# An encoder layer on one core: low parts of attention's weights on either engine, gates and fillers re-spread, the last two heads kept on chip, and the last projection's products in another order

## The chip, the cores and the metric
One Trainium2 chip, one of its cores. The metric is the device time of one execution in microseconds; the kernel's times are medians of several runs on the same chip.

## The reference
One layer of a streaming encoder, for 1024 prompt tokens and 32 new tokens that continue a cache of 512 (together T = 1056 token columns), model width 1024, 8 + 8 heads of 64, feed-forward width 4096, all in float32.

```python
h = rmsnorm(x)
z = h @ w_in                       # q,k,v of mixer A; indexer q,k,w; q,k,v of mixer B; gate_a, gate_b
# mixer A, per head: softmax(q k^T / 8) v over the top 256 keys that the indexer picks (a mask)
# mixer B, per head: a = exp(log_sigmoid(s) - sum of softplus(s) of the later keys); a v, causal
m = sigmoid(gate_a) * (o_a @ w_branch_a) + sigmoid(gate_b) * (o_b @ w_branch_b)
y = x + m @ w_out                  # then, with u = relu(rmsnorm(y) @ w_up) ** 2:
out = y + u @ w_down
```

## The kernel before
Every float32 product is made of three products of float32r parts: each operand x is split into a high part xh (a ScalarE cast) and a low part xl = x - xh (a subtraction), and `three` adds wh xh + wh xl + wl xh in one PSUM bank. A piece of weights is 128x512: `unit` loads it into `wst`, `split` makes `wh` on ScalarE and `wl` on the engine that `self.low` names. That is GpSimd from the start, and "either" from the feed-forward on.

The kernel doesn't issue instructions in the order of its code. `Plan` records each one with a rank (FAST, PREP, MAIN, FILL, SLOW) and then issues by its own estimated clock: on each engine the ready instruction of the lowest rank goes first. For an instruction of "either" it compares when VectorE and when GpSimd would be done with it (VectorE gets it if it would be done over 500 ns sooner: `dve + LEAN < pool`). What it decides is fixed in the program, so each engine runs its list in order and waits where the estimate was too early.

The stages, in the order of time, with the microsecond of the profile at which each begins: projections, indexer and top-k (0), mixer B's attention (465), mixer A's (685), merge with the gates (912), w_out (936), w_up (1029), w_down (1359).

Attention goes head by head (`attend`): two queries' blocks of scores (`s` banks), weights from them on ScalarE, VectorE and GpSimd, transposes (`t` banks), and products with v (`o` banks). `halves` adds the two halves of an `o` bank on ScalarE and VectorE into a tile `o`, which a DMA stores to `do` in HBM. Mixer A goes through its eight heads twice: pass 0 for the first 512 queries, pass 1 for the rest. A head's k, v and q come from HBM into rings of 3, 3 and 2 tiles. The few queries of the new tokens go with heads 2 and 5 (`attend_new`).

Between heads TensorE is given fillers (rank FILL, bank `pj`): gates (`gate`, 72 matmuls each, two pieces of `w_g`), and the branch products of finished heads, `branch_b0`, `branch_b1` and `branch_a0` (12, 24 and 12 matmuls). Four tables say how many are recorded where: `GATES_FIRST` ahead of mixer B's first head, `GATES_BESIDE[h]` behind B's head h, `FILL_AHEAD` ahead of mixer A, and `FILL_BESIDE` behind each head of A, pass 0 first. Fillers of A are held until the head before them is done (`behind`). The first `branch_b0` comes with `load_o`, which reads B's outputs from `do`. The last `load_o` brings A's outputs of the second half into `xl` for the merge.

The last projection (`down`) makes seven products per quarter of the output, by a scheme that saves one of eight. The inner dimension has 16 pieces of u. A stage goes over four quarters q; in its first quarter it loads the forms of u that it needs (`load`: a DMA, a cast on ScalarE, a subtraction on either engine, 128x528 each) into a ring of 24 slots, and keeps them for the other three. The stages are, in order: B11 (16 forms), the trio T2, T3, B22 over the first 8 pieces (24 forms) and over the other 8 (24 forms), B21 (16 forms), and the pair T1, T4 over 8 and 8 pieces (16 forms each). One unit is 24 matmuls: 4 pieces by two column blocks of 256 and 272 by 3 products. The trio's weights are sums and differences that VectorE makes (`us<-us`). `finish` multiplies a ready block, adds the residual from `dh` (ring `self.hs`) and stores it.

Of the kernel before, what the change touches and what calls it, by code (L numbers as in the profile page):

```python
# [10 lines left out]
F32 = mybir.dt.float32  # L11
# [12 lines left out]
SEQ = 1024  # L24
DEC = 32
PAST = 512
T = SEQ + DEC
# [19 lines left out]
GATES_BEFORE, GATES_FIRST = 4, 4  # L47
GATES_BESIDE = (1,1,1,1,1,1,0,0)
FILL_BESIDE = (0,1,1,1,2,2,2,2,2,2,2,2,2,2,2,1)
# [58 lines left out]
class Plan:  # L108
# [3 lines left out]
    def __init__(self, nc, tc):  # L112
        self.nc, self.tc = nc, tc
        self.tensor, self.vector = Issuer(self, PE, nc.tensor), Issuer(self, DVE, nc.vector)
        self.scalar, self.gpsimd = Issuer(self, ACT, nc.scalar), Issuer(self, POOL, nc.gpsimd)
        self.sync = Issuer(self, SP, nc.sync)
        self.either = Issuer(self, EITHER, nc)
        self.nodes, self.mem, self.rings = [], {}, {}
        self.members, self.banks, self.onchip = {}, set(), set()
# [31 lines left out]
    def open(self, name, side="left", space=None):  # L151
# [6 lines left out]
        self.members[name] = []  # L158
        return p
# [9 lines left out]
    def tile(self, pool, shape, dtype, name, tag=None, bufs=1, fine=False):  # L169
# [8 lines left out]
        if kw:  # L178
# [3 lines left out]
            m = Mem(1 if psum else 4, 1 if psum else words, old, self.floors[pool[2]])  # L182
# [277 lines left out]
class Layer:  # L460
# [103 lines left out]
    def run(self):  # L564
# [98 lines left out]

        self.att = self.pr = nc.open("att", "right")
# [542 lines left out]
    def attend(self, h, is_a, passes=(0, 1)):  # L1207

        nc, at = self.nc, self.att
        g = h if is_a else H + h  # L1210
        kk = nc.tile(at, [128, SEQ], F32R, "k", bufs=3)
# [27 lines left out]
        for i in passes:  # L1239
            o = nc.tile(at, [64, 512], F32, "o", bufs=2)  # L1240
            for t0 in (4 * i + 2, 4 * i):
# [22 lines left out]
                self.halves(po, o[:, c:c + 256])  # L1264
            with nc.rank(FAST):
                nc.sync.dma_start(self.do[g, :, 512 * i:512 * i + 512], o)
# [82 lines left out]
    def load_o(self, o, g, groups):  # L1349

        nc = self.nc
        for e in range(4):
            for i in groups:
                lo, hi = ((0, W1), (W1, T))[i]
                h, l = o[i][:, e], o[i][:, 4 + e]
                with nc.rank(PREP):
                    nc.sync.dma_start(
                        l.bitcast(F32), self.do[2 * g + 2 * e:2 * g + 2 * e + 2, :, lo:hi].rearrange("g e t -> (g e) t"))
                    nc.scalar.copy(h, l.bitcast(F32))
                    nc.gpsimd.tensor_sub(l, l.bitcast(F32), h.bitcast(F32))  # L1360
# [275 lines left out]
    def down(self, late, form):  # L1636
# [7 lines left out]
        self.hs = self.ring(self.temps(self.ft, 4, 0, 512))  # L1644
# [61 lines left out]
        for fs, weights, blocks, after in (  # L1706
                ((B11,), one(0, 0), (range(16),), after1),
                ((T2, T3, B22), weights6, (range(8), range(8, 16)), after6),
                ((B21,), one(0, 1), (range(16),), after2),
                ((T1, T4), weights5, (range(8), range(8, 16)), after5)):  # L1710
            for b, block in enumerate(blocks):
                u = {}
                for q in range(4):
                    tags = [next(self.turn) for _ in fs]
                    ps = [[self.bank(t)[:, :n] for n, _ in QUADS] for t in tags]
                    for p0, ws in [(p0, weights(q, p0 // 4)) for p0 in range(block[0], block[-1], 4)]:
                        for f, w, bank in zip(fs, ws, ps):
                            wh, wl = w()
                            if q == 0:
                                u.update({(f, p): load(f, p) for p in range(p0, p0 + 4)})  # L1720
                            for i, (n, lo) in enumerate(QUADS):
                                cs = slice(i * 256, i * 256 + n)
                                with nc.rank(FILL):
                                    for s in range(4):
                                        ks = slice(s * 128, s * 128 + 128)
                                        uh, ul = (z[:, cs] for z in u[f, p0 + s])
                                        self.three(bank[i], wh[:, ks], wl[:, ks], uh, ul,
                                                   p0 + s == block[0], p0 + s == block[-1])
                    for i, (n, lo) in enumerate(QUADS):

                        def d(r, c, done=False, q=q, n=n, lo=lo):
                            cs = slice(lo + c * n, lo + c * n + n)
                            if done:
                                return self.finish(2 * q + r, cs)
                            return self.pick(self.yy, 2 * q + r, cs)

                        with nc.rank(FAST):
                            after(b, d, *(z[i] for z in ps))
# [96 lines left out]
```

## Time and profile before

| | us |
|---|---|
| median of 3 runs (1704.97 to 1709.24) | 1705.32 |
| the profiled execution | 1703.88 |
| its span, first to last instruction | 1702.1 |
| TensorE busy with matmuls in the span | 1671.8 (98%) |
| VectorE, ScalarE, GpSimd busy | 1349.7, 942.4, 847.7 |

A matmul's busy time runs from its start to a modelled end and is longer than the time until the next may start, so a busy share near 100% doesn't say that TensorE issues at its pace. The share of its weight loads (PEld) falls with every wait, and so does the number of matmuls in a window of fixed length. L440 is the one line in which `Plan` issues everything, so instructions are told apart by their tiles: out<-in.

### The profile page before, as it was taken

The page shows a single profiled execution, that of the slowest core. Times are in us where ns is not written, and L with a number is a line of the kernel's source. Part 1 is how long each engine was busy: PE and PEld are TensorE (multiplying, and loading weights), DVE is VectorE, ACT ScalarE, POOL GpSimd, SP SyncE. Part 2 cuts the span into 40 slices and gives each one's busy share as a digit, 9 for nine tenths or more (in the row PEclk, how much of TensorE's full clock was granted, in tenths as well). Part 3 has the DMA queues.
Part 4 walks back from the last instruction along what each step waited for, and adds up shares of the span by engine and source line. Part 5 has one row for each costly group of instructions (what it writes and reads, how often), then busy time and mean ns, then how long its engine had stood idle before and what let it go on. Part 6 is the DMA issues. An engine that isn't in the chain of part 4 may idle for free.

```text
span 1702.1 us, 34820 instructions
## 1 busy us (share of the span) xinstructions
PE 1671.8 (98%) x12242; PEld 1591.3 (93%) x12242; DVE 1349.7 (79%) x2846; ACT 942.4 (55%) x2019; POOL 847.7 (50%) x699
## 2 busy tenths in 40 slices
PE   8999999999999999899999999999999999999998
PEld 7998999999999998798999999999999999989998
DVE  8777899987477888876666549999988879888756
ACT  7556888764376776877754555333333544425431
POOL 5432332343386676456668648433333556656420
PEclk9999999999999999999999999999999999999999
DMA  7234453355573636778855644444443687756744
GB/s 257 83 104 125 140 154 121 103 157 149 156 213 94 188 97 166 197 237 241 241 178 160 182 122 134 156 140 140 140 150 130 225 274 237 271 161 235 252 131 149
DMA packets 182575, 289.00 MB, mean 170 GB/s; under 512 B 30976, under 2 KB 62176, under 8 KB 182400
## 3 DMA queue, kind: packets, MB, share of 16 engines
q1 hardware_dynamic: 182112, 286.43, 54.4%
q8 instruction: 97, 1.59, 0.4%
q14 instruction: 78, 0.64, 0.1%
q10 hardware_dynamic: 288, 0.34, 0.1%
HBM read 193.52 MB, written 93.07 MB: 168 GB/s over the span
## 4 chain that ended last, share of the span: by engine, by line
PE 85%; DVE 8%; issue 2%; DMA 2%; ACT 1%; POOL 1%; SPq 0%; DVEq 0%; ACTq 0%; POOLq 0%
PE pj L440 35%; PE c L440 11%; PE b L440 10%; PE a L440 10%; PE s L440 10%; PE o L440 5%; PE t L440 5%; DVE junk L440 2%; DVE y L440 1%; DVE mh L440 1%; DVE us L440 1%; POOL wl L440 0%; SPq L440 0%; DVE wl L440 0%; DVE small L440 0%
## 5 line engine op out<-in xcount | busy, mean ns | idle before, releaser
L440 PE MATMUL pj<-xl,wh 128*128 128x272 f32 (+2 forms) x1200 | 335.5, 312 | 0.0
L440 POOL TENSOR_TENSOR wl<-wst,wh 128x512 fp32r<-128x512 f32 x160 | 231.5, 1455 | 200.8 <-ACT wh L440 195.1
L440 PE MATMUL pj<-xh,wh 128*128 128x272 f32 (+1 forms) x768 | 251.6, 328 | 0.0
L440 PE MATMUL pj<-xh,wl 128*128 128x272 f32 (+1 forms) x768 | 250.8, 327 | 0.2 <-POOL wl L440 0.2
L440 PEld LDWEIGHTS pj<-xl,wh 128*128 128x128 f32 x1200 | 212.9, 188 | 10.5
L440 ACT CAST wh<-wst 128x512 fp32r<-128x512 f32 x213 | 130.4, 620 | 132.0 <-PE a L440 21.9
L440 PEld LDWEIGHTS pj<-xh,wl 128*128 128x128 f32 x768 | 144.5, 188 | 11.1 <-POOL wl L440 0.5
L440 PEld LDWEIGHTS pj<-xh,wh 128*128 128x128 f32 x768 | 144.6, 188 | 10.2 <-DVE gz L440 0.3
L440 POOL TENSOR_TENSOR p<-p,rem 128x383 f32<-128x383 f32 (+8 forms) x66 | 101.8, 1562 | 45.3 <-DVE rem L440 34.3
L440 DVE TENSOR_TENSOR tt<-t,tt 128x512 fp32r<-128x512 f32 (+2 forms) x168 | 101.4, 621 | 26.4 <-ACT tt L440 25.5
L440 POOL TENSOR_TENSOR wl<-y,wh 128x512 fp32r<-128x512 f32 x49 | 73.2, 1496 | 95.9 <-ACT wh L440 92.8
L440 DVE TENSOR_TENSOR_SCAN rem<-rem,first 128x384 f32<-128x384 f32 (+8 forms) x66 | 113.9, 1748 | 7.5 <-ACT rem L440 6.3
L440 ACT CAST tt<-t 128x512 fp32r<-128x512 f32 (+2 forms) x168 | 86.9, 539 | 42.0 <-PE t L440 34.6
L440 ACT CAST wh<-y 128x512 fp32r<-128x512 f32 x79 | 49.1, 622 | 105.9 <-issue 23.0
L440 ACT ACTIVATE junk<-score,cand 128x1024 bf16<-128x1024 f32 (+2 forms) x93 | 97.0, 1043 | 12.3 <-DVE cand L440 10.7
L440 PE MATMUL s<-k,q 128*128 128x512 f32 (+4 forms) x384 | 97.9, 353 | 5.6 <-DVE nb L440 3.0
L440 ACT CAST wh<-us 128x512 fp32r<-128x512 f32 x64 | 39.6, 622 | 114.1 <-PE pj L440 27.6
L440 PE MATMUL o<-tt,v 128*128 128x256 f32 (+1 forms) x640 | 98.4, 279 | 0.8 <-DVE o L440 0.4
L440 PEld LDWEIGHTS o<-tt,v 128*128 128x128 f32 x640 | 89.9, 189 | 6.3 <-DVE o L440 0.7
L440 DVE TENSOR_SCALAR_CACHE_REDUCE junk<-score,cand 128x384 bf16<-128x384 f32 (+1 forms) x124 | 92.9, 749 | 3.1
L440 PE MATMUL t<-ident,p 128*128 128x128 f32 (+1 forms) x596 | 90.9, 275 | 0.2 <-DVE tt L440 0.2
L440 POOL TENSOR_TENSOR wl<-us,wh 128x512 fp32r<-128x512 f32 x33 | 49.7, 1515 | 72.6 <-ACT wh L440 72.6
(359 smaller groups left out, 5610.3 us busy)
## 6 DMA issues: line engine op xcount, KB each, us to landing
us<-w_down SPq DMA_DIRECT2D x80, 256.0 KB, 3.0
q<-dq SPq DMA_DIRECT2D x64, 256.0 KB, 4.5
du<-y SPq DMA_DIRECT2D x56, 264.0 KB, 2.5
du<-us SPq DMA_DIRECT2D x56, 264.0 KB, 2.5
y<-w_up SPq DMA_DIRECT2D x44, 256.0 KB, 2.7
k<-dk SPq DMA_DIRECT2D x40, 256.0 KB, 5.0
v<-dv SPq DMA_DIRECT2D x40, 256.0 KB, 4.3
xl<-du SPq DMA_DIRECT2D x35, 264.0 KB, 5.2
```

What stands on the lines that cost most here:

```text
L440: fn(*args, **kw)
```

## The change
1. `self.low` is "either" from the start of attention on, so the order maker puts the low parts of these weights (and of the cached v, `vcs`) on GpSimd or VectorE.
2. One gate fewer is recorded ahead of mixer B, two beside its first head, one beside heads 1 to 6. That leaves one gate instead of two for mixer A's fillers, and `FILL_BESIDE` begins with 1, 1, 1, 1, 1 instead of 0, 1, 1, 1, 2.
3. In pass 1 of mixer A the sums of the last two heads go into a tile `last` (in v's ring) instead of `o`, `do` and back; `load_o` takes the last quarter of the merge's input from there and loads only the new tokens' 32 columns.
4. The order maker's estimate of when a PSUM pool is free is that of the pool's opening.
5. `self.hs` has 9 slots of 272 columns instead of 4 of 512, and `down` goes B11, trio, B21, trio, pair, pair.

```diff
-GATES_BEFORE, GATES_FIRST = 4, 4
-GATES_BESIDE = (1,1,1,1,1,1,0,0)
-FILL_BESIDE = (0,1,1,1,2,2,2,2,2,2,2,2,2,2,2,1)
+GATES_BEFORE, GATES_FIRST = 4, 3
+GATES_BESIDE = (2,1,1,1,1,1,1,0)
+FILL_BESIDE = (1,1,1,1,1,2,2,2,2,2,2,2,1,2,2,1)
...
+        self.low = nc.either
         self.att = self.pr = nc.open("att", "right")
...
-    def halves(self, po, o):
+    def halves(self, po, o, out=None):
...
-        nc.vector.tensor_add(o, po[0:64], o)
+        nc.vector.tensor_add(o if out is None else out, po[0:64], o)
...
+        direct = is_a and passes[0] == 1 and h >= H - 2
+        if direct and h == H - 2:
+            self.last = nc.tile(at, [128, SEQ], F32, "last", tag="v", bufs=3)
...
-            with nc.rank(FAST):
-                nc.sync.dma_start(self.do[g, :, 512 * i:512 * i + 512], o)
+            if not direct:
+                with nc.rank(FAST):
+                    nc.sync.dma_start(self.do[g, :, 512 * i:512 * i + 512], o)
...
+                x, old = l.bitcast(F32), 0
+                if g == 0 and i == 1 and e == 3:
+                    x, old = self.last[:, :T - W1], SEQ - W1
...
-        self.hs = self.ring(self.temps(self.ft, 4, 0, 512))
+        self.hs = self.ring(self.temps(self.ft, 9, 0, 272))
...
-        for fs, weights, blocks, after in (
-                ((B11,), one(0, 0), (range(16),), after1),
-                ((T2, T3, B22), weights6, (range(8), range(8, 16)), after6),
-                ((B21,), one(0, 1), (range(16),), after2),
-                ((T1, T4), weights5, (range(8), range(8, 16)), after5)):
...
+        three, two = ((T2, T3, B22), weights6, after6), ((T1, T4), weights5, after5)
+        for (fs, weights, after), b, block in (
+                (((B11,), one(0, 0), after1), 0, range(16)), (three, 0, range(8)),
+                (((B21,), one(0, 1), after2), 0, range(16)), (three, 1, range(8, 16)),
+                (two, 0, range(8)), (two, 1, range(8, 16))):
```

Up to the start of mixer B's attention, and in the whole of w_up, TensorE's order is the same in both kernels; both have 12,238 matmuls. Three places show what else moved.

TensorE in pass 0 of mixer A, from the second pair of scores of head 3 to the first pair of head 4's first block; `pj` rows are fillers. Before:

```order
L440 MATMUL s<-k,q 128x384 x2
L440 MATMUL o<-tt,v 128x256
L440 MATMUL o<-tt,v 128x128 x2
L440 MATMUL t<-ident,p 128x128 x6
L440 MATMUL s<-k,q 128x512 x2
L440 MATMUL s<-k,q 128x128 x2
L440 MATMUL s<-k,q 128x256 x2
```

And now:

```order
L441 MATMUL s<-k,q 128x384 x2
L441 MATMUL pj<-xl_104,wh_6911 128x512
L441 MATMUL o<-tt,v 128x256
L441 MATMUL o<-tt,v 128x128 x2
L441 MATMUL t<-ident,p 128x128 x3
L441 MATMUL pj<-xh_103,wl_6912 128x512
L441 MATMUL t<-ident,p 128x128 x3
L441 MATMUL pj<-xh_103,wh_6911 128x512
L441 MATMUL pj<-xl_104,wh_6911 128x512
L441 MATMUL s<-k,q 128x512 x2
L441 MATMUL s<-k,q 128x128 x2
```

Matmuls of a gate now stand among a head's transposes and products where there was none. From the first scores of head 1 to those of head 6 the order before has 7 fillers, all behind head 5's first scores; now it has 11, 8, 8, 9 and 30 behind the first scores of heads 1 to 5.

ScalarE at the end of the trio's first stage in `down`; `wh` are weights, `ml`, `oa`, `xl`, `mh` the forms of the next stage in the ring's slots. Before:

```order
L440 CAST wh_13339<-us_12757 128x512
L440 CAST ml_12644<-ml_12644 128x528
L440 CAST wh_13347<-us_12756 128x512
L440 CAST oa_12640<-oa_12640 128x528 x2
L440 CAST wh_13349<-us_12756 128x512
L440 CAST oa_12640<-oa_12640 128x528
L440 CAST oa_12641<-oa_12641 128x528
L440 CAST wh_13351<-us_12756 128x512
L440 CAST oa_12641<-oa_12641 128x528 x3
```

And now:

```order
L441 CAST wh_13340<-us_12758 128x512
L441 CAST ml_12645<-ml_12645 128x528
L441 CAST wh_13345<-wst 128x512
L441 CAST oa_12641<-oa_12641 128x528 x3
L441 CAST wh_13348<-wst 128x512
L441 CAST oa_12641<-oa_12641 128x528 x2
L441 CAST wh_13351<-wst 128x512
L441 CAST oa_12642<-oa_12642 128x528 x2
```

The forms that are made there now belong to B21, and the weights beside them come straight from HBM (`wst`) and no longer from VectorE's sums (`us`). The trio's second stage stands 16 forms later, and 8 of its 24 forms are cast during B21, beside the weights of its second quarter.

ScalarE at the end of mixer A; `o` is the copy of the last head's half bank, `gz` the sigmoid of a gate. Before:

```order
L440 CAST wh_7652<-wst 128x512
L440 COPY o<-o 64x256
L440 CAST wh_7700<-wst 128x512
L440 ACT_TABLE_LOAD
L440 ACTIVATE gz<-gz 128x512
L440 CAST xl_106<-xl_106 128x544
```

And now:

```order
L441 CAST wh_7653<-wst 128x512
L441 COPY o<-o 64x256
L441 ACT_TABLE_LOAD
L441 ACTIVATE gz<-gz 128x512
L441 CAST xl_106<-last 128x544
```

The cast for the merge now reads the tile `last` that VectorE writes instead of what a DMA brought back. On TensorE 17 branch matmuls of 512 columns stand between the last product with v and the merge's first now, 47 before.

## Rows read from the trace of the kernel before

**Rows 1.** The page's first part: engine, busy us (share of the span), instructions.

```profile
PE 1671.8 (98%) x12242; PEld 1591.3 (93%) x12242; DVE 1349.7 (79%) x2846; ACT 942.4 (55%) x2019; POOL 847.7 (50%) x699
```

**Rows 2.** Busy time by window: two windows in mixer B, then from head 1's to head 6's first scores in pass 0 of mixer A. Columns: window, its length, busy us (instructions) of PE, PEld, DVE, ACT, POOL, then granted clock, DMA share, GB/s.

```profile
500.00:550.00 50.00, 50.00 (x351) 46.69 (x350) 40.35 (x64) 36.11 (x83) 36.75 (x25) 1.00 0.29 80
600.00:650.00 50.00, 50.00 (x357) 47.00 (x356) 40.76 (x65) 36.42 (x87) 39.40 (x27) 1.00 0.51 139
691.40:718.00 26.60, 22.45 (x147) 18.67 (x147) 24.69 (x107) 24.71 (x64) 12.23 (x21) 1.00 0.81 209
```

**Rows 3.** The same view of four stages of `down`: trio, trio, B21 and the first pair.

```profile
1409.08:1479.37 70.29, 70.29 (x578) 70.29 (x577) 60.06 (x70) 27.71 (x48) 41.33 (x27) 1.00 0.69 231
1479.37:1556.55 77.18, 72.94 (x578) 72.03 (x577) 63.32 (x82) 29.87 (x52) 44.01 (x28) 0.98 0.65 220
1556.55:1603.39 46.84, 46.84 (x386) 46.84 (x385) 34.57 (x45) 19.08 (x31) 21.34 (x14) 1.00 0.65 218
1603.39:1650.20 46.81, 46.81 (x386) 46.81 (x385) 32.40 (x49) 19.44 (x33) 19.03 (x12) 1.00 0.57 192
```

**Rows 4.** The timeline of TensorE at the first scores of heads 4, 5 and 6 in pass 0, with the idle time before them in brackets; SyncE's issues of the two loads of q, 256 KB each, for heads 5 and 6 (start, and the time that both issues took); a window as in rows 2; and the time from issue to landing of the six loads of q from 704 to 719.

```profile
707.05 1.26 PE L440 MATMUL s<-k,q 128*128 128x384 f32 x6
712.12 0.59 PE L440 MATMUL s<-k,q 128*128 128x384 f32 x2 [1.62 <-DVE nb L440]
718.05 0.59 PE L440 MATMUL s<-k,q 128*128 128x384 f32 x2 [1.40 <-DVE nb L440]
...
705.72 1.25 SPq L440 DMA_DIRECT2D q<-dq  x2
710.16 1.23 SPq L440 DMA_DIRECT2D q<-dq  x2
...
710.00:715.00 5.00, 3.38 (x24) 2.92 (x24) 3.97 (x20) 4.17 (x12) 3.29 (x5) 1.00 1.05 292
...
DMA to landing us min/median/max: 3.9/5.0/7.0
```

**Rows 5.** The trio's second stage: what TensorE waited for from 1479.37 to 1512 (us in total, times, longest), then VectorE, GpSimd and ScalarE in the timeline (start, us, engine, what, idle before), the first row of VectorE and of GpSimd from ahead of the crowded stretch, and a window with the granted clock.

```profile
PE c L440 <- ACT wh L440: 1.8, 1, 1.8
PE pj L440 <- ACT wh L440: 1.3, 1, 1.3
...
1467.11 0.71 DVE L440 TENSOR_TENSOR ml<-ml 128x528 fp32r<-128x528 f32 x1 [0.94 <-ACT ml L440]
1486.40 5.32 DVE L440 TENSOR_TENSOR mh<-mh 128x528 fp32r<-128x528 f32 x3
1500.29 6.81 DVE L440 TENSOR_TENSOR us<-us 128x512 f32<-128x512 f32 x4
...
1469.00 4.74 POOL L440 TENSOR_TENSOR oa<-oa 128x528 fp32r<-128x528 f32 x3 [4.83 <-ACT oa L440]
1489.36 5.27 POOL L440 TENSOR_TENSOR mh<-mh 128x528 fp32r<-128x528 f32 x3
...
1499.52 1.22 ACT L440 CAST wh<-us 128x512 fp32r<-128x512 f32 x2 [9.77 <-DVE us L440]
...
1502.00:1514.00 12.00, 11.25 (x80) 11.25 (x81) 11.26 (x12) 3.61 (x6) 6.33 (x5) 0.86 0.66 211
```

**Rows 6.** Low parts of weights: duration in ns (min/median/max) and first and last start of those on GpSimd and on VectorE in the whole kernel; GpSimd's group of them from 465 to 900 (busy us, mean ns, idle time before them and what ended it); and what TensorE waited for one of them, in the whole kernel.

```profile
L440 POOL TENSOR_TENSOR wl<-wst,wh x160: 1267/1298/3280, 10.5 to 1611.1; 128x512 fp32r<-128x512 f32 x160
L440 DVE TENSOR_TENSOR wl<-wst,wh x53: 675/693/1809, 1016.5 to 1680.2; 128x512 fp32r<-128x512 f32 x53
...
L440 POOL TENSOR_TENSOR wl<-wst,wh 128x512 fp32r<-128x512 f32 x45 | 70.3, 1573 | 52.4 <-ACT wh L440 48.5 <-PE t L440 3.1 <-issue 0.3
...
PE pj L440 <- POOL wl L440: 0.2, 1, 0.2
```

**Rows 7.** The timeline at the end of mixer A: the last head's sum on ScalarE and VectorE, its store and its load, ScalarE's and GpSimd's work on it, and TensorE at a filler and at the merge's first product.

```profile
901.51 0.37 ACT L440 COPY o<-o 64x256 f32<-64x256 f32 x1
901.92 0.42 DVE L440 TENSOR_TENSOR o<-o 64x256 f32<-64x256 f32 x1 [0.63 <-ACT o L440]
902.36 0.47 SPq L440 DMA_DIRECT2D do<-o  x1
904.68 0.32 SPq L440 DMA_DIRECT2D xl<-do  x1
906.21 1.28 ACT L440 ACT_TABLE_LOAD   x1 [2.05 <-DMA gz<-dg]
907.50 0.64 ACT L440 ACTIVATE gz<-gz 128x512 f32<-128x512 f32 x1
908.04 0.63 ACT L440 CAST xl<-xl 128x544 fp32r<-128x544 f32 x1
908.75 1.37 POOL L440 TENSOR_TENSOR xl<-xl 128x544 fp32r<-128x544 f32 x1 [0.15 <-ACT xl L440]
...
904.86 0.62 PE L440 MATMUL pj<-og,wh 128*128 128x512 f32 x2
905.54 0.62 PE L440 MATMUL pj<-og,wh 128*128 128x512 f32 x2
911.81 0.41 PE L440 MATMUL a<-xl,wh 128*128 128x272 f32 x2
```

More of the change, by code (lines that the diff above doesn't have):

```diff
@@ L118, in __init__ @@
         self.nodes, self.mem, self.rings = [], {}, {}
-        self.members, self.banks, self.onchip = {}, set(), set()
+        self.members, self.banks, self.onchip, self.under = {}, set(), set(), {}
         self.floors = {"left": 0.0, "right": 0.0, None: 0.0}
@@ L158, in open @@
         self.members[name] = []
+        self.under[name] = self.floors[side if space is None else None]
         return p
@@ L181, in tile @@
             psum = pool[3].startswith("ps") and not fine
-            m = Mem(1 if psum else 4, 1 if psum else words, old, self.floors[pool[2]])
+            m = Mem(1 if psum else 4, 1 if psum else words, old, self.under[pool[3]] if pool[3].startswith("ps") else self.floors[pool[2]])
             ring.append(m)
@@ L1263, in attend @@
                                 start=j + z == 0, stop=j + z == t0 + 2)
-                self.halves(po, o[:, c:c + 256])
-            with nc.rank(FAST):
-                nc.sync.dma_start(self.do[g, :, 512 * i:512 * i + 512], o)
+                self.halves(po, o[:, c:c + 256], self.last[h % 2 * HD:h % 2 * HD + HD, c:c + 256] if direct else None)
+            if not direct:
+                with nc.rank(FAST):
+                    nc.sync.dma_start(self.do[g, :, 512 * i:512 * i + 512], o)
             self.mid = self.mid[1:] + [len(nc.nodes) - 1]
@@ L1355, in load_o @@
                 h, l = o[i][:, e], o[i][:, 4 + e]
+                x, old = l.bitcast(F32), 0
+                if g == 0 and i == 1 and e == 3:
+                    x, old = self.last[:, :T - W1], SEQ - W1
                 with nc.rank(PREP):
                     nc.sync.dma_start(
-                        l.bitcast(F32), self.do[2 * g + 2 * e:2 * g + 2 * e + 2, :, lo:hi].rearrange("g e t -> (g e) t"))
-                    nc.scalar.copy(h, l.bitcast(F32))
-                    nc.gpsimd.tensor_sub(l, l.bitcast(F32), h.bitcast(F32))
+                        x[:, old:], self.do[2 * g + 2 * e:2 * g + 2 * e + 2, :, lo + old:hi].rearrange("g e t -> (g e) t"))
+                    nc.scalar.copy(h, x)
+                    nc.gpsimd.tensor_sub(l, x, h.bitcast(F32))
     def branch(self, name, e, o, done, parts):
@@ L1704, in after5 @@
                     d(r, c, True)
-        for fs, weights, blocks, after in (
-                ((B11,), one(0, 0), (range(16),), after1),
-                ((T2, T3, B22), weights6, (range(8), range(8, 16)), after6),
-                ((B21,), one(0, 1), (range(16),), after2),
-                ((T1, T4), weights5, (range(8), range(8, 16)), after5)):
[L1711 to L1738, printed above, removed]
@@ new lines, in down, with d @@
+        three, two = ((T2, T3, B22), weights6, after6), ((T1, T4), weights5, after5)
[3 more added lines that the diff above has]
+                (two, 0, range(8)), (two, 1, range(8, 16))):
+            u = {}
+            for q in range(4):
+                tags = [next(self.turn) for _ in fs]
+                ps = [[self.bank(t)[:, :n] for n, _ in QUADS] for t in tags]
+                for p0, ws in [(p0, weights(q, p0 // 4)) for p0 in range(block[0], block[-1], 4)]:
+                    for f, w, bank in zip(fs, ws, ps):
+                        wh, wl = w()
+                        if q == 0:
+                            u.update({(f, p): load(f, p) for p in range(p0, p0 + 4)})
+                        for i, (n, lo) in enumerate(QUADS):
+                            cs = slice(i * 256, i * 256 + n)
+                            with nc.rank(FILL):
+                                for s in range(4):
+                                    ks = slice(s * 128, s * 128 + 128)
+                                    uh, ul = (z[:, cs] for z in u[f, p0 + s])
+                                    self.three(bank[i], wh[:, ks], wl[:, ks], uh, ul,
+                                               p0 + s == block[0], p0 + s == block[-1])
+                for i, (n, lo) in enumerate(QUADS):
+                    def d(r, c, done=False, q=q, n=n, lo=lo):
+                        cs = slice(lo + c * n, lo + c * n + n)
+                        if done:
+                            return self.finish(2 * q + r, cs)
+                        return self.pick(self.yy, 2 * q + r, cs)
+                    with nc.rank(FAST):
+                        after(b, d, *(z[i] for z in ps))
```

## The prediction
> **What bounds the kernel now.** I read the page's first part, then windows by stage, then TensorE's waits and the timeline around them. TensorE is the bound: its matmuls cover 98% of the span and its weight loads 93% [rows 1]. So nothing off TensorE is worth anything unless it ends a wait of TensorE, and the question is where it waits. Two ways show it. In `down`, stages of the same work can be laid side by side: the trio's two stages have 578 matmuls each, and take 70.29 and 77.18 us; B21 and the first pair take 46.84 and 46.81 [rows 3]. So the trio's second stage holds 6.9 us of waiting, and the others next to none. In attention, weight loads fill 93 to 94% of a stretch without waits (46.69 of 50.00, 47.00 of 50.00), but 18.67 of 26.60 us between head 1 and head 6 in pass 0 of mixer A [rows 2]. At 93.4% the 18.67 us would have taken 20.0, so 6.6 us are lost there. These are the two places with a sum behind them. Low parts of weights on GpSimd are not: TensorE waited for one of them for 0.2 us in the whole kernel [rows 6].
>
> **Why TensorE waits at these two places.** In pass 0 a head is 8 score matmuls, 10 transposes and 12 products with v. Five heads took 26.6 us, 5.3 each; of that, weight loads were 3.7 each [rows 2]. Heads 4, 5 and 6 begin at 707.05, 712.12 and 718.05, so 5.1 and 5.9 apart. SyncE issues the two loads of q for head 5 from 705.72 to 706.97 and for head 6 from 710.16 to 711.39; such a load takes 3.9 to 7.0 us to land, with the DMA engines full (1.05) [rows 4]. For head 6 the longest one ends where the scores begin: about 710.8 + 7.0 = 717.8. The waits are put down to VectorE's `nb`, but the loads fit the times. VectorE is not far behind: 24.69 of 26.60 us [rows 2]. So the heads go by at about 5.3 us each, whatever TensorE could do, and there was nothing else for it to do.
>
> In the trio's second stage VectorE and GpSimd get in each other's way. A subtraction of a form takes VectorE 0.71 us alone and 1.77 in the crowd (5.32 for 3), GpSimd 1.58 and 1.76 (4.74 and 5.27 for 3). All 24 slots are in use by the stage before, so 24 forms have to be made in the time in which the slots come free. VectorE comes to the next weights' sums late, ScalarE waits 9.77 us for them, and TensorE for ScalarE 1.8 and 1.3 [rows 5]. In the window behind it the granted clock is 0.86, a part of it at the lower of the two levels, 1.2 GHz instead of 2.4; TensorE had just waited.
>
> **The change, part by part.**
>
> *Order of `down`.* The trio's second stage now follows B21. B21 needs 16 of the 24 slots, so 8 of the trio's forms can be made during B21, and 16 are left for the crowded stretch. B21 itself gets its 16 forms with no slot free ahead, as it did before, where it took 46.84 us, no more than the pair's 46.81 with 8 slots free [rows 3]. The pair now has no slot free ahead of it either, but that is B21's old place with as many forms and no sums on VectorE. The trio with 8 slots ahead is the trio's old first stage: 70.29. So the four stages should come out at 70.3, 46.8, 70.3 and 46.8. The gain is between 0 (the wait only moves) and 6.9; I take 6.4 and leave half a microsecond for VectorE's three-step `finish` in B21, which stands ahead of the trio where B11 had only copies on ScalarE.
>
> *Fillers in pass 0.* Counted over heads 1 to 5, the order now has 66 fillers where there were 7. At the steady pitch of 0.23 us for 512 columns (three in 0.68 us [rows 7]) and 0.12 for about 264 (a unit of 24 in 70.29 / 24 = 2.93 us [rows 3]) the 66 are 10.9 us, the 7 were 1.4. With 20.0 us for what was there before, TensorE has 29.5 us of work for five heads that can pass in 26.6: it becomes the bound. As the number of matmuls is unchanged, the 9.5 us are taken from other places that were full. The gain lies between 0 and 6.6. Spread by heads it isn't even: heads 1 to 4 have 11, 8, 8 and 9 fillers, about 1.5 us each, which on top of a head's 3.8 is just the old pace of 5.3. There a late q still shows, the more so as its ring has two tiles and the scores that free one are now spread by fillers. So I take 5.0.
>
> *What pass 1 loses.* Those fillers are missing later. Before, fillers in pass 1 were plenty enough that weight loads and matmuls ran through; heads there have two to three times the matmuls of pass 0. I take 0.6 us of new waits for it, bounds 0 and 3 (half the loss of pass 0).
>
> *Low parts on either engine.* By the two orders 42 of them go from GpSimd to VectorE between the start of attention and w_up: 10 in mixer B, 14 in mixer A, 18 in merge and w_out. One takes VectorE between 0.69 us (median) and 1.81 (longest) [rows 6], so 29 to 76 us more over some 560 us. VectorE is 81 to 82% busy in mixer B [rows 2]; 10 more are 7 to 18 us in 220, and bring it to 84 to 90%. TensorE waits for neither: nothing gained beyond the 0.2 us above, and nothing lost as long as VectorE isn't late with scans and `tt`. If that cover is gone, it is the rival below. On the other side GpSimd's queue no longer holds the products of weights and sums (`p`) behind a low part.
>
> The Trainium skill, page "SBUF — State Buffer", section "Who interferes with whom", speaks against this edit: a VectorE instruction with two SBUF inputs and a GpSimd instruction that reads SBUF contend, and the one that comes second is blocked until the first is finished. By that rule each moved subtraction that meets one on GpSimd would take 1.30 + 0.69 = 1.99 us. The trace agrees in kind and is a little milder: 1.77 in the crowd [rows 5], at most 1.81 for a low part [rows 6]. By the rule VectorE's share in mixer B would end at 90% too, so the sum is the same by either.
>
> *The last two heads.* Before, the last head's sum was ready at 902.3, stored, loaded again, and in ScalarE's hands at 908.04; TensorE was on fillers until 911.81 [rows 7]. So the round trip of 5.7 us cost nothing. Now 17 fillers are left behind the last product (17 x 0.23 = 3.9 us), and nine merge matmuls that don't need the last heads (1.1): 5.0 us. In that time come ScalarE's copy (0.37), the table load (1.28) and a sigmoid (0.64) that stand ahead in ScalarE's queue, and the cast (0.63): 2.9 us; GpSimd's 1.37 more has until 5.9. In the trace the table load waited 2.05 us for a gate from HBM [rows 7]; with that it is 5.0 against 5.0, and 6.4 against 5.9. I take 0.3 us, bounds 0 and 1.
>
> *The rest.* The planner's estimate of a PSUM pool only changes the order, which is counted above. `finish` with more slots for the residual: TensorE waited for none of it in B21 or the pair [rows 3]. The order of w_up is unchanged.
>
> **The sum.** The profiled execution took 1703.88, 1.8 more than its span. Less 6.4 and 5.0, plus 0.6 and 0.3: 1693.4. The median of the runs is 1.4 above that execution, so 1695 for a median.
>
> **Rivals.**
> 1. *Pass 0 is paced by something that the fillers don't cover.* The new fillers include branch products, whose weights, gate and store are three transfers of 256 KB for 2.8 us of TensorE, and the DMA engines are already full there [rows 4]. Heads then pass at 6 us or more and fillers wait for weights. Against it: up to head 6's q the two orders issue about the same (some 5.8 MB from head 2's q on). Only `down` gains: 1695 + 5.0 = 1700.
> 2. *The wait in `down` only moves*, to the pair or B21, because in the crowd VectorE and GpSimd together finish two forms per 1.77 us, 16 in 14 us, and a quarter of B21 lasts 11.7. Against it stands B21's 46.84. Then 1695 + 6.4 = 1701.4.
> 3. *Both*: 1706.4, no change.
> 4. *Slower: low parts at the head of VectorE's queue.* GpSimd stood idle 52.4 us ahead of 45 low parts, 48.5 of it for ScalarE's cast [rows 6], 1.2 us each, without harm. On VectorE the same wait holds up scans, `tt` and maxima behind it: 24 in attention at 1.16 + 1.81 are 71 us on an engine with 40 us to spare in 220 of mixer B and 2 of 26.6 in pass 0. If more than 17 of the 71 us reach TensorE, the gains are gone and 5 more: 1711 to 1725.
>
> **How the numbers follow.** The forecast gets 0.62, rivals 1 to 4 get 0.16, 0.09, 0.05 and 0.08. A measurement can tell about 0.3%, 5 us, from no change, so faster means below 1700.2, slower above 1710.4. Of rival 1 a little over half is below that line, of rival 2 a third; the forecast whole: 0.62 + 0.09 + 0.03 = 0.74. Same: 0.07 + 0.06 + 0.05 = 0.18; slower 0.08. The forecast's own range, 1690 to 1698, comes from its bounds: 6.9 and 6.6 in full without new waits give 1691.8, on a median that may lie 1 or 2 us off; 6.4, half of the second gain and 2 us of new waits give 1697.6. For 8 in 10 it has to take in the first two rivals: 1688 to 1702. Outside are rivals 3 and 4 and a little below.
>
> **What the profile would show.** Right: the trio's second stage, now behind B21, within a microsecond of 70.3, and the clock at 1.00 in it; weight loads at 90% or more between head 1 and head 6 of pass 0, with 66 or so more matmuls there; the longest waits of TensorE those of the start. Wrong: TensorE waiting for `mh`, `ml` or `wh` in B21 or the first pair (rival 2); idle rows ahead of `s<-k,q` or of `pj` in pass 0 with the DMA share at 1 (rival 1); VectorE waiting for ScalarE's `wh` in mixer B and TensorE for `tt` or `rem` (rival 4); TensorE idle ahead of the merge's second product (the last heads).

## The result and the profile after

The changed kernel takes 1696.71 us (median of 4 runs, 1694.51 to 1697.95) where the kernel before takes 1705.26 (1704.97 to 1709.24): a ratio of 0.9941, 95% interval 0.9926 to 0.9956. The profiled execution took 1694.51 us, its span is 1692.7. Run again later beside three experiments (e5_changed, below), it took 1694.15, ratio 0.9930 (0.9917 to 0.9942). The forecast was 1695. One execution of e11 and one of e12 (below) took 3290.76 and 4172.47 us, for a cause that nothing here shows; no median, range or ratio below counts them, and as e11's profile is of that execution, no stage of e11 is read.

The page's first part and two groups of the changed kernel, to be held against [rows 1] and [rows 6]:

```profile
PE 1668.0 (99%) x12242; PEld 1590.7 (94%) x12242; DVE 1380.0 (82%) x2896; ACT 947.6 (56%) x2025; POOL 792.9 (47%) x649
...
L441 POOL TENSOR_TENSOR wl<-wst,wh 128x512 fp32r<-128x512 f32 x121 | 174.3, 1447 | 191.5 <-ACT wh L441 166.2
...
L441 DVE TENSOR_TENSOR wl<-wst,wh 128x512 fp32r<-128x512 f32 x92 | 85.8, 937 | 38.2 <-ACT wh L441 37.5
```

39 low parts have moved (160 and 53 before, 121 and 92 now), and VectorE stands 37.5 us ahead of low parts waiting for ScalarE's casts. VectorE's group in the kernel before, and what VectorE waited for ahead of low parts in the changed kernel's attention (465 to 912):

```profile
L440 DVE TENSOR_TENSOR wl<-wst,wh 128x512 fp32r<-128x512 f32 x53 | 46.9, 890 | 29.2 <-ACT wh L440 29.0
...
DVE wl L441 <- ACT wh L441: 4.7, 3, 2.0
```

So 29.0 of the 37.5 us were there before, and attention has 4.7 of them.

Busy time by window, columns as in [rows 2]: head 1's to head 6's first scores in pass 0, then B11, the first trio, B21, the second trio and the first pair:

```profile
692.10:719.50 27.40, 27.40 (x200) 25.73 (x199) 23.74 (x101) 26.27 (x60) 8.44 (x16) 1.00 0.84 233
1352.03:1404.22 52.19, 49.34 (x386) 48.49 (x385) 39.16 (x45) 23.31 (x46) 23.92 (x15) 0.97 0.85 288
1404.22:1474.52 70.30, 70.30 (x579) 70.30 (x577) 60.46 (x72) 29.04 (x49) 38.48 (x25) 1.00 0.68 230
1474.52:1521.91 47.39, 47.03 (x387) 46.82 (x386) 38.08 (x45) 20.78 (x34) 27.12 (x18) 1.00 0.72 236
1521.91:1594.02 72.11, 70.45 (x578) 70.25 (x577) 61.37 (x78) 27.73 (x47) 42.15 (x27) 1.00 0.66 227
1594.02:1640.83 46.81, 46.81 (x386) 46.81 (x385) 33.24 (x50) 19.76 (x34) 19.86 (x12) 1.00 0.55 185
```

and the same of B11 in the kernel before:

```profile
1359.49:1409.08 49.59, 47.90 (x387) 47.05 (x386) 39.21 (x43) 23.67 (x47) 26.55 (x17) 1.00 0.87 290
```

From head 1 to head 6 of pass 0 weight loads fill 25.73 of 27.40 us (94%) where they filled 18.67 of 26.60 [rows 2]. The second trio is down from 77.18 [rows 3] to 72.11, not to 70.3; B21 is up from 46.84 to 47.39; and B11, on which the prediction's sum had no term, is up from 49.59 to 52.19.

The table shows where TensorE lost time. A matmul's loss is the time from its start to the next one's, less the median of that for its form in the whole kernel; the losses are summed by stage. Of the changed kernel the two profiled executions are given.

| loss of TensorE, us | before | changed, twice | the prediction's change |
|---|---|---|---|
| up to mixer B | 14.9 | 15.0, 14.7 | 0 |
| mixer B | 4.4 | 4.3, 3.9 | 0 |
| mixer A, pass 0 | 7.9 | 1.3, 1.5 | -5.0 |
| mixer A, pass 1 | 3.4 | 2.1, 2.3 | +0.6 |
| merge, w_out | 0.4 | 0.5, 0.5 | +0.3 |
| w_up | 3.2 | 3.3, 3.3 | 0 |
| B11 | 2.9 | 5.5, 4.1 | 0 |
| second trio | 7.2 | 2.1, 2.2 | -6.9 |
| B21 | 0.2 | 0.7, 0.8 | +0.5 |
| the rest of down | 0.7 | 0.7, 0.7 | 0 |
| sum | 45.3 | 35.7, 33.9 | -10.5 |

So the sum came out, and its terms didn't: `down` gave 1.9 (3.2 in the second execution) instead of 6.4, attention (mixer B and both passes of mixer A) 8.1 instead of 4.4.

What TensorE waited for in B11 of the changed kernel and in that of the kernel before (us in total, times, longest), and rows of the changed kernel's timeline around that wait; the last row is a window of 6 us behind it:

```profile
PE a L441 <- POOL wl L441: 2.3, 1, 2.3
...
PE a L440 <- DVE wl L440: 1.2, 1, 1.2
...
1367.44 0.63 ACT L441 CAST wh<-wst 128x512 fp32r<-128x512 f32 x1
1368.62 3.52 POOL L441 TENSOR_TENSOR oa<-oa 128x528 fp32r<-128x528 f32 x2
1370.39 0.62 ACT L441 CAST wh<-wst 128x512 fp32r<-128x512 f32 x1 [2.32 <-DMA wst<-w_down]
1370.95 0.65 PE L441 MATMUL a<-mh,wh 128*128 128x256 f32 x4
1372.11 3.42 POOL L441 TENSOR_TENSOR wl<-wst,wh 128x512 fp32r<-128x512 f32 x2
1373.89 0.58 PE L441 MATMUL a<-mh,wl 128*128 128x256 f32 x1 [2.29 <-POOL wl L441]
...
1373.00:1379.00 6.00, 5.11 (x30) 5.12 (x31) 5.15 (x5) 0.00 (x0) 2.52 (x2) 0.72 0.68 218
```

GpSimd makes two forms of the first trio (`oa`) and only then the low part that TensorE's next product needs. It belongs to the stage's seventh piece of weights: 148 products of the stage stand ahead of the wait, six pieces of 24 and four of this one, the row at 1370.95. These four use the high part already, while the cast at 1370.39, for which ScalarE waited 2.32 us, ends at 1371.01; so the seventh piece's cast is the one at 1367.44, done at 1368.07, and its low part stood 4 us behind forms on GpSimd, not behind a load. Before, VectorE made this low part, and TensorE waited 1.2 us. Behind the wait the granted clock is 0.72, so a part of these 6 us went at 1.2 GHz.

### The profile page after: what moved, and what is told of

The parts are those of the page before. It is cut to its first block, busy times and chain, and to the rows that moved or that the text cites. A ratio compares the mean times of both kernels' runs of the same rounds, so it can differ in the third digit from the quotient of the medians.

```text
span 1692.7 us, 34767 instructions
## 1 busy us (share of the span) xinstructions
PE 1668.0 (99%) x12242; PEld 1590.7 (94%) x12242; DVE 1380.0 (82%) x2896; ACT 947.6 (56%) x2025; POOL 792.9 (47%) x649
## 4 chain that ended last, share of the span: by engine, by line
PE 83%; DVE 7%; DMA 5%; issue 2%; POOL 2%; ACT 1%; SPq 0%; ACTq 0%; DVEq 0%; POOLq 0%
PE pj L441 33%; PE b L441 10%; PE s L441 10%; PE c L441 10%; PE a L441 10%; PE t L441 5%; PE o L441 5%; DVE junk L441 2%; DVE y L441 1%; DMA xl<-du 1%; DMA q<-dq 1%; DMA wst<-w_down 1%; POOL wl L441 1%; DVE xl L441 1%; SPq L441 0%
## 5 line engine op out<-in xcount | busy, mean ns | idle before, releaser
L441 POOL TENSOR_TENSOR wl<-wst,wh 128x512 fp32r<-128x512 f32 x121 | 174.3, 1447 | 191.5 <-ACT wh L441 166.2
L441 POOL TENSOR_TENSOR p<-p,rem 128x383 f32<-128x383 f32 (+8 forms) x66 | 111.7, 1711 | 52.3 <-DVE rem L441 29.8
L441 DVE TENSOR_TENSOR wl<-wst,wh 128x512 fp32r<-128x512 f32 x92 | 85.8, 937 | 38.2 <-ACT wh L441 37.5
L441 DVE TENSOR_TENSOR_SCAN rem<-rem,first 128x384 f32<-128x384 f32 (+8 forms) x66 | 108.0, 1658 | 2.2 <-ACT rem L441 1.5
```

The lines of the kernel that those rows point to most:

```text
L441: fn(*args, **kw)
```

## Experiments: one part of the change at a time

The first three add one part of the change to the kernel before; they ran on one chip, beside the kernel before at 1705.5 us.

**e1_tables**: the three tables alone (the diff's first six lines).

> The kernel before with only the new tables of gates and fillers. TensorE's order has 8, 10, 11, 23 and 24 fillers behind the first scores of heads 1 to 5 in pass 0 of mixer A, where the kernel before has 0, 0, 0, 0 and 7. Between the first scores of pass 0 and those of pass 1 the kernel before loses 7.9 us against TensorE's steady pitch, the changed kernel 1.3. Theory A (fillers cover what the heads wait for): the loss falls to 1.5 or less, weight loads fill over 90% from head 1 to head 6, and the time falls by 5 to 8 us, to 1697 to 1700. Theory B (the changed kernel gained there because low parts of weights left GpSimd, whose products of weights and sums then came sooner): heads 2 to 5 go on waiting, the loss stays above 5, and the time is 1703 to 1706. Down is that of the kernel before in both: 49.6, 70.3, 77.2, 46.8, 46.8, 46.9.

Measured: 1702.94 us, ratio 0.9983 (0.9974 to 0.9991). From head 1 to head 6, and what TensorE waited for behind the last product with v:

```profile
693.70:724.80 31.10, 30.44 (x218) 28.42 (x217) 23.72 (x95) 28.74 (x61) 10.50 (x17) 1.00 0.77 204
...
PE pj L440 <- POOL wl L440: 3.8, 1, 3.8
```

Weight loads fill 91%, and the loss of pass 0 is 1.0: theory A, as far as pass 0 goes. But the time fell by 2.6 and not by 5 to 8, since the merge, without a wait before, now has one of 3.8 us and loses 5.5 in all; in the 6 us behind the wait the granted clock is 0.76. Behind the last product with v only 27 fillers are left of 47.

**e2_either**: the line `self.low = nc.either` alone.

> The kernel before with only the low parts of attention's weights on either engine. Fillers behind the first scores of heads 1 to 5 of pass 0: 10, 0, 0, 1 and 8. Theory A (fillers): heads 2 to 5 have next to none and still lose 5 us or more in pass 0; the time is 1703 to 1706, the same. Theory B (GpSimd's queue): the loss of pass 0 falls below 2 us and the time to 1697 to 1700. Slower rival of the prediction (low parts at the head of VectorE's queue hold up scans): 1707 or more, with TensorE waiting for tt or rem in mixer B.

Measured: 1700.60 us, ratio 0.9968 (0.9955 to 0.9982). Neither theory: pass 0 still loses 5.7, with waits for q, `tt`, `mx` and `wh`; and yet the time is 4.9 us lower, with the loss lower in small pieces (mixer B 4.4 to 2.8, pass 0 7.9 to 5.7, pass 1 3.4 to 2.3). The slower rival is out.

**e3_down**: the order of `down` and the nine slots of the residual.

> The kernel before with only the new order of down and the nine slots of 272 columns for the residual. Attention is that of the kernel before. Both theories expect the trio's second stage at 72 us, 5 less than 77.2, and B21 at 47.4. In the changed kernel B11 took 52.2 us instead of 49.6, and one low part of its second quarter's weights, the seventh, is made by GpSimd and no longer by VectorE. Theory P (that choice of the order maker costs it: GpSimd has two forms ahead of it): B11 takes 52 here too, and the time falls by 2, to 1703. Theory N (weights that landed late in that execution by chance): B11 takes 49.6, and the time falls by 4.5, to 1700.7.

Measured: 1703.44 us, ratio 0.9988 (0.9980 to 0.9997). B11 and the second trio:

```profile
1367.38:1419.60 52.22, 49.41 (x386) 48.55 (x385) 39.16 (x45) 23.48 (x46) 23.89 (x15) 0.97 0.86 290
1537.31:1609.43 72.12, 70.45 (x579) 70.25 (x577) 61.15 (x78) 27.76 (x47) 41.39 (x27) 1.00 0.68 227
```

Theory P: the low part on GpSimd costs B11 the same here, with the granted clock down to 0.97 again, and 2.1 us is all that `down` brings. The profiled execution is the highest of the twelve (1709.87), so only its stages of `down` are read.

The next four ran together on another chip (kernel before: 1706.2): the changed kernel, and that kernel less one part.

**e5_changed**:

> The changed kernel once more, on one chip with the next three, and as a measure of how far its stages differ from execution to execution: 1695 to 1698; pass 0 of mixer A loses 1.0 to 1.6 us, B11 takes 52.2 and the trio's second stage 72.1.

Measured: 1694.15 us (1693.02 to 1695.57), a little below what was expected. B11, and the 6 us behind its wait, which is 2.3 us long again:

```profile
1351.86:1402.60 50.74, 47.92 (x386) 47.07 (x385) 38.85 (x45) 23.29 (x46) 23.62 (x15) 1.00 0.88 296
...
1373.00:1379.00 6.00, 5.27 (x43) 5.27 (x44) 5.19 (x6) 0.89 (x2) 2.38 (x2) 1.00 0.64 158
```

B11 took 50.7 here and not 52.2: the clock stayed at 1.00. So of B11's 2.6 us, 1.1 are the longer wait and 1.5 the clock that fell behind it in one execution and not in the other.

**e6_no_either**: without `self.low = nc.either`.

> The changed kernel with the low parts of attention's weights on GpSimd alone, as before. With the tables alone TensorE lost 1.0 us in pass 0, but 3.9 us in one piece at the 35th product or so of the merge, where a low part of weights on GpSimd came late: it stood behind four sums of the merge, and weights' loads stood behind the last head's store and load on SyncE. Theory G (GpSimd's queue in the merge is the cause): the same wait of 3 to 5 us is here too, and the time is 1699 to 1702. Theory R (the last head's way through HBM is the cause): no wait over 1 us in the merge, and the time is that of the changed kernel within 2 us, 1695 to 1698, as pass 0 and down are the same.

Measured: 1695.51 us, ratio 0.9943 (0.9930 to 0.9955), and no wait in the merge at all. That is 1.4 above the changed kernel, but the two intervals overlap, so these runs don't show that 1.4 clear of noise. Theory R so far: GpSimd's queue alone doesn't make that wait.

**e7_no_direct**: the last two heads through HBM.

> The changed kernel with the last two heads by way of HBM again, 24 fillers behind the last product with v (17 in the changed kernel, 47 in the kernel before). Theory R (the way through HBM was what the tables uncovered): the merge loses 3 to 5 us more than in the changed kernel, 1699 to 1702. Theory G: nothing, within 1.5 us of the changed kernel; 24 fillers of 0.23 us and 1.1 us of the merge are 6.6 us against a round trip of 5.7.

Measured: 1699.16 us, ratio 0.9959 (0.9945 to 0.9973), 5.0 above. What TensorE waited for in the merge, and the way there on SyncE, ScalarE and GpSimd; the last row is ScalarE's in the changed kernel:

```profile
PE pj L441 <- POOL wl L441: 3.3, 1, 3.3
...
898.27 0.47 SPq L441 DMA_DIRECT2D do<-o  x1
900.52 0.32 SPq L441 DMA_DIRECT2D xl<-do  x1
900.93 1.77 SPq L441 DMA_DIRECT2D wst<-w_ba  x3
...
903.66 0.65 ACT L441 CAST xl<-xl 128x544 fp32r<-128x544 f32 x1 [2.88 <-DMA xl<-do]
904.21 4.27 ACT L441 CAST mh<-y 128x512 fp32r<-128x512 f32 x8
908.39 1.66 ACT L441 CAST wh<-wst 128x512 fp32r<-128x512 f32 x3
...
908.90 3.83 POOL L441 TENSOR_TENSOR ft<-ft,y 128x272 f32<-128x272 f32 x4 [1.91 <-DVE ft L441]
912.69 4.59 POOL L441 TENSOR_TENSOR wl<-wst,wh 128x512 fp32r<-128x512 f32 x3
...
903.08 1.66 ACT L441 CAST wh<-wst 128x512 fp32r<-128x512 f32 x3
```

Theory R. The last head itself is in time. What is late stands behind it: SyncE holds its queue until the head's store has landed, three loads of weights come after that, their casts behind eight others, and their low parts behind four sums of the merge. In the changed kernel these casts begin at 903.08, and no wait follows. The wait is 3.3 us and the merge loses 5.1 more; the granted clock is 0.72 in the 6 us from 914.

**e8_no_tables**: the old tables.

> The changed kernel with the old tables of gates and fillers. Low parts alone brought the kernel before from 1705.5 to 1700.6, tables alone to 1702.9 (and 4 us of what they brought were given back in the merge); all parts together brought 8.8. Theory O (tables and low parts each end the same waits in part, so they don't add up): attention as with the low parts alone, where pass 0 still lost 5.7 us, and down as in the changed kernel: 1700.6 less 2, about 1698.5, 2 above the changed kernel. Theory S (they add up): the changed kernel plus the 6.6 that tables end in pass 0: 1703.

Measured: 1697.59 us, ratio 0.9952 (0.9939 to 0.9964), 3.4 above. Pass 0 loses 5.6, as with the low parts alone: nearer to theory O. Together:

| part | alone, against before | taken out of the changed kernel |
|---|---|---|
| tables | -2.6 | +3.4 |
| low parts on either | -4.9 | +1.4, not clear of noise |
| order of down, nine slots | -2.1 | not run |
| last heads direct | not run | +5.0 |
| estimate of PSUM pools | not run | not run |

Tables and low parts end the same waits in part. And the direct last heads, for which the prediction had +0.3, are what the tables need: these take the fillers away that had hidden the round trip.

## Experiments: what holds the heads of pass 0, B11 and the second trio

**e9_no_q_loads**: on the kernel before,

```diff
+                if passes == (0,) and h > 0:
+                    qs[i] = self.q0
...
+                    continue
                 qs[i] = nc.tile(at, [128, 2, 512], F32R, "q", bufs=2)
+                self.q0 = qs[i]
```

> The kernel before, with the q of head 0 used by all eight heads of pass 0 of mixer A: seven pairs of loads of q are left out, so mixer A's first half is computed with a wrong q. The fillers behind heads 1 to 5 are as before (0, 0, 0, 0, 7). Theory Q, that of the prediction (heads pass at 5.3 us because q's loads land late): from head 1 to head 6 VectorE and ScalarE were busy 24.7 us of 26.6, so the five heads pass in 24.7 to 25.2, and the loss of TensorE in pass 0 falls from 7.9 to about 6. Theory V (VectorE, ScalarE and GpSimd hand a head's work to each other at that pace, and q is there or not): 26 us or more as before, and the loss stays above 7.

Measured: 1706.13 us, ratio 0.9998 (0.9989 to 1.0007). Windows from head 1 to head 4 and from head 4 to head 6:

```profile
691.90:707.60 15.70, 14.74 (x100) 12.39 (x100) 15.02 (x63) 14.72 (x38) 5.59 (x11) 1.00 0.36 92
707.60:715.60 8.00, 7.74 (x50) 6.54 (x50) 7.83 (x37) 7.88 (x21) 4.97 (x8) 1.00 0.54 179
```

and the same two of the kernel before:

```profile
691.40:707.10 15.70, 14.71 (x100) 12.37 (x100) 15.01 (x63) 14.72 (x38) 5.62 (x11) 1.00 0.71 181
707.10:718.00 10.90, 7.74 (x48) 6.30 (x48) 9.68 (x45) 10.00 (x27) 6.61 (x11) 1.00 0.97 248
```

Each theory has its half. Heads 1 to 3 take 15.70 us with and without the loads: VectorE is busy 15.0 of it. Heads 4 and 5 take 8.0 instead of 10.9, so the five take 23.7, less than theory Q said. The trace of the kernel before shows that q was late there: the second load of head 5's q, issued at 706.35, landed 5.6 us later, at 712.0, and that of head 6's at 717.8; their scores begin at 712.12 and 718.05. In heads 1 to 4 the scores begin 0.5 to 2.1 us behind the landing. How much of the 2.9 us is q itself and how much the traffic that went with it (DMA share 0.97 and 0.54), the run doesn't part. The loss of pass 0 fell to 4.9, and that of pass 1 to 1.9; the merge gave it back, with 28 fillers behind the last head and a loss of 6.2, the wait of e1 and e7.

**e4_slots4**: the changed kernel with `self.hs = self.ring(self.temps(self.ft, 4, 0, 512))`; it ran with e1 to e3.

> The changed kernel with the old ring of four slots of 512 columns for the residual. In its order the seventh low part of B11 is on VectorE again, as in the kernel before. Theory P: B11 takes 49.6 instead of 52.2, and the time is 2.6 below the changed kernel's, about 1694 (0.9935 of the kernel before instead of 0.995). Theory N: B11 as in the changed kernel on average, 1696.7. Should four slots be too few for the three-step finish, VectorE waits for loads of the residual in B21 and B21 takes longer than 47.4.

Measured: 1692.92 us, ratio 0.9923 (0.9911 to 0.9935). B11:

```profile
1352.88:1402.50 49.62, 47.87 (x387) 47.02 (x385) 39.48 (x43) 23.61 (x47) 27.22 (x17) 1.00 0.86 291
```

Theory P. A ring that TensorE never waits for costs 1.1 us (2.6 with the clock), as its size changes which engine the order maker picks for one low part. B21 took 47.39: four slots are enough.

**e10_forms_held**: on the changed kernel, in `down`,

```diff
+        mark = [None]
...
+            if len(fs) == 1 and block[0] == 0 and mark[0] is None:
+                first = True
...
+            wait = mark[0] if len(fs) == 3 and b == 0 else None
             for q in range(4):
+                if first and q == 1:
+                    mark[0] = len(nc.nodes) - 1
...
-                            u.update({(f, p): load(f, p) for p in range(p0, p0 + 4)})
+                            with nc.held(wait):
+                                u.update({(f, p): load(f, p) for p in range(p0, p0 + 4)})
```

> The changed kernel, where the order maker lets the loads of the first trio's forms start only behind B11's first quarter. In B11 five of these forms stood on VectorE and GpSimd ahead of the low part that TensorE waited 2.4 us for, and their loads beside that of the weights. Theory P (the low part is late because of them): B11 takes 47 to 48.5 us instead of 50.7 (52.2 where the clock fell behind the wait), and the time is 2.5 to 4 below the changed kernel's 1694.2 to 1696.7. Rival D (the weights themselves land late, whatever stands on the two engines: ScalarE waited 2.3 us for them): B11 stays at 50 or more. A cost could appear where these forms are now made, in B11's other quarters or at the trio's start: then the first trio takes more than 70.3.

Measured: 1691.52 us, ratio 0.9911 (0.9897 to 0.9925). B11 and the first trio, the one wait of TensorE in B11, VectorE at the low part of the seventh piece and of the next, and SyncE's issues of the loads of the seventh to ninth:

```profile
1350.98:1398.74 47.76, 47.09 (x387) 46.88 (x385) 35.95 (x44) 24.48 (x47) 23.82 (x16) 1.00 0.89 310
1398.74:1469.04 70.30, 70.30 (x579) 70.30 (x578) 59.79 (x71) 28.22 (x49) 39.49 (x26) 1.00 0.69 234
...
PE pj L441 <- DVE ml L441: 0.7, 1, 0.7
...
1363.57 2.42 DVE L441 TENSOR_TENSOR wl<-wst,wh 128x512 fp32r<-128x512 f32 x2
...
1356.59 3.16 SPq L441 DMA_DIRECT2D wst<-w_down  x3
```

Theory P: B11 takes 47.76, and the first trio pays nothing. The seventh low part is begun 12.6 us into the stage, where it was 20.1 in the changed kernel. By this run alone rival D could stand, as the edit lets the weights' loads go earlier too: that of the seventh piece is issued 5.6 us into the stage instead of 10.5 (1362.57). The changed kernel's own trace rules it out: there the seventh piece's cast was done 4 us before GpSimd came to its low part, and the 2.3 us that ScalarE waited were for the eighth.

**e11_finish_late**: on the changed kernel,

```diff
             add(d(0, 0), p2, d(0, 0))
-            d(0, 0, True)
+            with nc.rank(SLOW):
+                d(0, 0, True)
```

> The changed kernel with the three-step finish of B21's blocks at the lowest rank, so that the order maker puts it behind everything else that is ready. In the changed kernel VectorE is busy without a gap from 1522 to 1540 and comes late to the weights' sums of the second trio's second quarter; three steps of finish stand there at 1.56 us each. Theory F (these 4.7 us are what makes the sums late): the second trio takes 70.5 instead of 72.1, and the time falls by 1.5. Theory C (the crowd of 16 forms would do it alone, and finish only lands elsewhere): 72 as before.

Measured: 1690.70 to 1694.09 us in four executions, ratio 0.9923 (0.9908 to 0.9937): lower than the changed kernel by about as much as theory F says, but not clear of it by these runs alone.

**e12_both**:

> Both edits: forms of the first trio held, finish of B21 late. If both theories P and F hold, B11 at 48 and the second trio at 70.5: 4 to 5.5 us below the changed kernel, 1690 to 1692, below each version so far. If only P: 1692 to 1694.

Measured: 1687.55, 1687.59 and 1687.83 us, ratio 0.9891 (0.9876 to 0.9906): 18 us below the kernel before, the fastest of all, and 2.4 below the 1690 to 1692 expected: that sum had B11 and the trio in it, and B21 came down too. B11, B21 and the second trio, then B21 and the second trio of e10, which has the old `finish`:

```profile
1352.10:1399.87 47.77, 47.08 (x386) 46.88 (x385) 35.38 (x44) 24.35 (x47) 25.06 (x16) 1.00 0.91 313
1470.17:1516.93 46.76, 46.76 (x386) 46.76 (x385) 37.20 (x47) 21.15 (x34) 23.28 (x15) 1.00 0.70 231
1516.93:1587.35 70.42, 70.42 (x579) 70.27 (x577) 59.28 (x79) 28.31 (x47) 41.76 (x27) 1.00 0.71 236
...
1469.04:1516.44 47.40, 47.02 (x387) 46.82 (x386) 37.86 (x45) 21.12 (x35) 27.24 (x18) 1.00 0.68 229
1516.44:1588.53 72.09, 70.45 (x578) 70.25 (x577) 61.75 (x78) 28.09 (x47) 41.62 (x27) 1.00 0.69 232
```

Theory F: the second trio takes 70.42 where e10, which differs by `finish` alone, takes 72.09. ScalarE's first two casts of the second quarter's weights, in the changed kernel, with TensorE's one wait in that stage, and in e12, where TensorE has none:

```profile
1538.27 0.62 ACT L441 CAST wh<-us 128x512 fp32r<-128x512 f32 x1 [8.65 <-DVE us L441]
1540.83 1.30 ACT L441 CAST wh<-us 128x512 fp32r<-128x512 f32 x2 [1.93 <-DVE us L441]
...
PE c L441 <- ACT wh L441: 1.7, 1, 1.7
```

```profile
1530.97 0.62 ACT L441 CAST wh<-us 128x512 fp32r<-128x512 f32 x1 [6.05 <-DVE us L441]
1531.82 0.62 ACT L441 CAST wh<-us 128x512 fp32r<-128x512 f32 x1 [0.23 <-DVE us L441]
```

The first is 16.4 us and 14.0 us after the stage's start, the second, for which TensorE waited, 18.9 and 14.9. The crowd of 16 forms is the same; what made the sums late was `finish` of the block before.

## Why the prediction was right, point by point

- **The sum** was right, 1695 against 1696.71, and so was the sign, but that it came so close is luck: `down` brought 3.2 to 4.5 us less than forecast, attention 3.7 more.
- **Order of `down`, -6.4.** The mechanism was right: eight forms made ahead, ScalarE's first cast of the second quarter's weights 16.4 us into the second trio instead of 20.2 [rows 5], the clock at 1.00 there. The size was off: -5.1 in the trio, +0.5 in B21, +2.6 (+1.1) in B11, in all -1.9 (-3.2). Two steps failed. The half microsecond "for VectorE's three-step `finish` in B21" was 1.7 in the trio and 0.6 in B21, as e12 shows against e10 by moving `finish` alone. And "`finish` with more slots for the residual: TensorE waited for none of it" looked at the wrong place: the slots work through the order maker, on a low part in B11, two stages ahead of the first `finish` (e3, e4). Rival 2, that the wait only moves, fell: the half microsecond that B21 gained is `finish` again, and gone in e12 (46.76).
- **Fillers in pass 0, -5.0.** Measured -6.6 and -6.4 of the 7.9 that the whole pass lost, and next to nothing is left of the prediction's 6.6 from head 1 to head 6. The step that cut it to 5.0, that a late q would still show in heads 1 to 4, was wrong: q was late for heads 5 and 6 only (e9, and the landings in the kernel before). Nor did the new loads hold up the heads (rival 1). The Trainium skill, page "Perfetto Trace Analysis", section "Optimization Strategy", says that regimes with different limits may gain by being interleaved; the 94% of weight loads in pass 0 agree. But the work put there can be missed where it was before, as in the merge of e1. The sign of 66 or so more matmuls in that window was miscounted: 66 fillers for 7 are 59 more, and the window has 53 more in all, as some products with v moved out of it.
- **Pass 1, +0.6.** Measured -1.3 and -1.1. Its fillers were missed nowhere: with the tables alone pass 1 loses as much as before (e1), with the low parts alone 2.3 (e2). So the gain came with the low parts, as far as one execution of each shows.
- **Low parts on either engine, 0.** Alone they were worth 4.9 (e2), in the company of the other parts 1.4, which is not clear of noise (e6). The prediction asked what TensorE waits for by name and found 0.2 us for low parts; in e2 these are still 0.2, and what went from 473 to 905 are the waits for `nb` (3.0 us before, none now) and `rem` (1.0), while those for `tt` are 1.6 where they were 1.2. So what went are waits that don't bear the low parts' name. Whether the small waits went because GpSimd's queue is shorter or because the order maker put 19 fillers in place of 7 behind heads 1 to 5, these runs don't separate. Rival 4 fell: of its 71 us in attention 28 are VectorE waiting ahead of 24 low parts (24 x 1.16); it waited 4.7 there, and TensorE's waits for `tt` and `rem` from 473 to 900 fell from 2.2 to 1.0.
- **The last heads, +0.3.** Measured +0.1. But what the step is worth was read under the cover of the kernel before, 47 fillers, which another part of the same change takes away. Against what the changed kernel has, it is worth -5.0 (e7).

## What to carry to other kernels

Price an edit in the company of the edits beside it: a round trip that is free under 47 fillers costs 5 to 6 us under 24 to 28, whichever edit took the fillers (e1, e7, e9). Where an order maker decides, a change of a ring's size is a change of order: look through the new order around each wait that the trace already shows, not only where the ring is used. And what stands ahead of a late instruction on its engine is worth more than what it waits for: holding back forms that aren't needed yet, and finished blocks that nobody waits for, took another 0.39% off the time (ratios 0.9891 and 0.9930).

## What the runs showed of the hardware

The clock after a wait is not the same in every execution: behind the same wait of 2.3 us in B11 it was 0.72 over 6 us in one execution of the changed kernel and 1.00 in the other, and B11 took 52.19 and 50.74 us. The same wait stands in four more of the runs: in e3 the clock over B11 was 0.97 (52.22 us), in e6, e7 and e8 it was 1.00 (50.73, 50.76 and 50.69). A wait can so cost more than half as much again behind it, or nothing.
